# The stick-breaking mixer's logits from 64-row matmuls in pairs, copied from PSUM to SBUF before anything reads them

## The chip, the cores and the metric

The kernel runs on one NeuronCore of a Trainium2 chip. The metric is the device time of one launch in microseconds (us). The kernel before took 719.55 us (median of 3 runs, 719.12 to 720.17).

## The reference

One layer of a model on 512 tokens of width 1024, with 16 meta tokens ahead of them (528 keys). All numbers are float32. A projection by `w_in` feeds two mixers: a gated recurrence (`hgrn2`, 4 heads) and a stick-breaking attention (8 heads of width 64). Their outputs side by side go through `w_out`, then come a residual with layer norm, a mixture of 16 experts and a second layer norm. The part that is changed is this, for blocks of 128 queries:

```
z = einsum('bhqd,bhkd->bhqk', q[start:end] * 64**-0.5, k[:end])      # logits, 8 heads
log_keep = where(mask, log_sigmoid(-z), 0)
log_a = log_sigmoid(z) + cumsum(log_keep, reverse=True) - log_keep
a = where(mask, exp(log_a), 0)
o = einsum('bhqk,bhkd->bhqd', a, v[:end])
```

After it `h = layer_norm(ALPHA * h + mixed @ w_out)`.

## The kernel before

The work falls into stages: the projections and the recurrence (up to about 243 us), the stick-breaking mixer woven with the multiplication by `w_out` (to about 352 us), routing (to about 420 us), and the experts, whose weights stream in to the end.

**Large matmuls** are made as three: an operand is split into a high part (a copy on ACT, rounded) and a low part (the difference, on DVE or POOL), and `mm3` (L126 to L130) adds three products. For `w_out` the split is in `wo_half` (L711): a raw MB arrives by a DMA that SP issues (L716), ACT copies it (L725), and `lo_sub` (L124 on DVE, L122 on POOL) makes the low part. `out_proj` (L818) then makes 24 matmuls of 128x512 for each of four blocks of rows with the first half of `w_out`, and as many with the second half. They go to PSUM banks named `z`.

**The mixer** (`stick_breaking`, L568) takes its queries in three units: unit 0 is the block of the last 128 queries against 528 keys, unit 1 the block before it against 400 keys, unit 2 the first two blocks together (144 and 272 keys, 416 columns). Each unit goes through four pairs of heads. For each head `sb_weights` (L484) makes the logits in a PSUM bank `pj` (there are four of these), adds the mask by a small bf16 matmul, and then runs

```
ll = Abs(z)                    ACT  L504, reads PSUM
cc = max(z, 0)                 DVE  L508 (for 2 heads of 8 ACT, L506), reads PSUM
ll = Ln(1 + Exp(-ll))          ACT  L509, L510
cc = scan(cc + ll), reversed   DVE  L513
cc = z - cc                    DVE  L515, reads PSUM: the bank is held until here
cc = Exp(cc)                   ACT  L516
```

`sb_values` (L521) transposes the weights (L529), copies them out of PSUM on DVE (L531) and multiplies by the values (L536), one pair behind; `sb_finish` (L539) adds the meta tokens (L544, L548), normalizes, and transposes the result (L561). The queries lie in eight tiles `sqZ`, one for each head: 128 rows, of which 64 hold the head and 64 are zero, so that a matmul against the 128 rows of a pair of heads' keys takes the one head. `ev_sq` (L386) fills them: eight memsets on POOL (L393), four scaled copies on DVE (L397) and four on ACT (L395).

**What sets the order.** The program is written as generators that `weave` interleaves: 0.8 steps of `out_proj` to one step of `stick_breaking`. A scheduler then lays the instructions of each engine into a fixed order by when it believes each can run; on the chip each engine keeps that order. Large tiles (`big_tile`, 8 KB a partition) come from one pool of 14 buffers in the order of the program, and are reused in turn. The two tiles of `sqZ`, the tiles of `svt`, the gains `gb`, and the raw and split tiles of `w_out` all come from it. The first seven loads of expert weights (L879, from a pool of their own that becomes free when the recurrence is done) are issued by `pump` ahead of the weave; each load after the third waits until the load three before it has landed.

Of the kernel before, what the change touches and what calls it, by code (L numbers as in the profile page):

```python
# [13 lines left out]
AF = mybir.ActivationFunctionType  # L14
OP = mybir.AluOpType
# [3 lines left out]
P = 128  # L19
# [34 lines left out]
HG_LEAD = 2.0  # L54
WO_RATIO = 0.8
EARLY = 2
RELU_SHARE = 2
ZS_BUFS = 3
AT_BUFS = 2
T_BUFS = 2  # L60
# [21 lines left out]
def hymba_kernel(ctx: ExitStack, tc: tile.TileContext, x, meta, w_in, lbnd, hgg, sbg, w_out, ln1g, ln1b,  # L82
                 wrg, brg, wre, bre, wg, wu, wd, ln2g, ln2b, out):
    nc = tc.nc
    V = nc.vector
# [28 lines left out]
    def big_tile(k, dt=F32, pool=None):  # L114
        return (pool or big).tile([P, 2048], dt, tag="b", name="b").rearrange("p (k n) -> p k n", k=k)
# [46 lines left out]
    def tt(tag="t", bufs=T_BUFS, n=528, parts=P):  # L162
        return att.tile([P, 528], F32, tag=tag, bufs=bufs, name=tag)[0:parts, 0:n]
# [27 lines left out]
    for i2 in range(2):  # L191
        xr_ = xr[i2]
        for i1 in range(2):
            i = 2 * i2 + i1
# [25 lines left out]
    for m in (16, 8, 4, 2, 1):  # L220
        t = upool.tile([P, P], I32, tag=f"lm{m}", bufs=1, name=f"lm{m}")
# [9 lines left out]
    identb = att.tile([P, P], BF, name="identb")  # L231
    maskb = att.tile([P, P], BF, name="maskb")
# [136 lines left out]
            yield 1  # L369


    skT, sqZ, svt = [], [], []
    vbd = att.tile([P, 512], F32, name="vbd")

    def ev_sk(c, acc):
# [8 lines left out]
            V.tensor_copy(skT[c][:, 0:NM], p_[:, c, :])  # L384

    def ev_sq(c, acc):  # L386
        if c % 2 == 0:
            t = big_tile(4)
            sqZ.extend(t[:, j] for j in range(4))
        for s in range(2):  # L390
            q_ = sqZ[2 * c + s]
            r, o = slice(64 * s, 64 * s + 64), slice(64 * (1 - s), 64 * (1 - s) + 64)
            nc.gpsimd.memset(q_[o], 0.0)  # L393
            if s:
                nc.scalar.activation(q_[r], acc[r], AF.Copy, scale=0.125)  # L395
            else:
                V.tensor_scalar(q_[r], acc[r], 0.125, None, op0=OP.mult)  # L397

    def ev_sv(i, acc):
        if i == 0:  # L400
# [78 lines left out]
    UNITS = (((3,), ((0, 528),), 528, ((0, 1, 2, 3),)), ((2,), ((0, 400),), 400, ((0, 1, 2, 3),)),  # L479
             ((0, 1), ((0, 144), (144, 416)), 416, ((0, 1), (2,), (3,))))  # L480

    relu = [0]

    def sb_weights(pr, s, am, qts, spans, n):  # L484
        h = 2 * pr + s
        pieces = []
        if n == 528:
            for a in range(2):
                z = pj()
                nc.tensor.matmul(z[:, 0:264], sqZ[h][:, 384:512], skT[pr][:, 264 * a:264 * a + 264],  # L490
                                 start=True, stop=not a)
                pieces.append((z, 264 * a, 264))
            nc.tensor.matmul(z[:, 136:264], identb, maskb, start=False, stop=True)
        else:
            z = pj()
            for i, (a, b) in zip(qts, spans):
                nc.tensor.matmul(z[:, a:b], sqZ[h][:, i * P:(i + 1) * P], skT[pr][:, 0:b - a],
                                 start=True, stop=False)
                nc.tensor.matmul(z[:, b - P:b], identb, maskb, start=False, stop=True)
            pieces.append((z, 0, n))  # L500
        ll, cc = tt(), tt("zs", ZS_BUFS)
        relu[0] += RELU_SHARE
        for z, a, w in pieces:
            nc.scalar.activation(ll[:, a:a + w], z[:, 0:w], AF.Abs)  # L504
            if relu[0] // 8 != (relu[0] - RELU_SHARE) // 8:
                nc.scalar.activation(cc[:, a:a + w], z[:, 0:w], AF.Relu)  # L506
            else:
                V.tensor_scalar(cc[:, a:a + w], z[:, 0:w], 0.0, None, op0=OP.max)  # L508
        nc.scalar.activation(ll[:, 0:n], ll[:, 0:n], AF.Exp, scale=-1.0)  # L509
        nc.scalar.activation(ll[:, 0:n], ll[:, 0:n], AF.Ln, bias=1.0)  # L510
        for a, b in spans:
            rv = slice(b - 1, a - 1 if a else None, -1)
            V.tensor_tensor_scan(cc[:, rv], cc[:, rv], ll[:, rv], 0.0, op0=OP.add, op1=OP.add)  # L513
        for z, a, w in pieces:
            V.tensor_sub(cc[:, a:a + w], z[:, 0:w], cc[:, a:a + w])  # L515
        nc.scalar.activation(cc[:, 0:n], cc[:, 0:n], AF.Exp)  # L516
# [50 lines left out]

    def stick_breaking():  # L568
        todo = []
        st = {}  # L570

        def drain():
            pr, qts, spans, prs, am, bank_, zz = todo.pop(0)
            if pr == prs[0]:
                st["o"] = bank_()
            sb_values(prs.index(pr), pr, prs, st["o"], zz, qts, spans)
            if pr == prs[-1]:
                sb_finish(am, st["o"], prs, qts)

        for qts, spans, n, groups in UNITS:  # L580
            for g, prs in enumerate(groups):
                am = att.tile([P, 2, P], F32, tag="am", bufs=3, name="am")
                if len(prs) < 4:
                    nc.gpsimd.memset(am, 0.0)
                for m, pr in enumerate(prs):
                    zz = []
                    for s in range(2):
                        zz.append(sb_weights(pr, s, am, qts, spans, n))
# [670 lines left out]
    for e in range(NE):  # L1259
        acc = [pj(), pj()]  # L1260
# [53 lines left out]
    rows = rr + list(oth)  # L1314
# [103 lines left out]
```

## Time and profile before

| what | value |
|---|---|
| median of the runs | 719.55 us (719.12 to 720.17) |
| profiled execution, its own time | 718.7 us |
| span of its trace | 717.0 us |
| PE busy | 656.4 us, 92% |
| DVE busy | 540.7 us, 75% |
| ACT busy | 425.5 us, 59% |
| DMA, mean over the span | 200 GB/s |

The profiled execution lies 1.7 us over its span and 0.85 us under the median. Busy shares over the whole span mix stages with different limits, so the stage from 243 to 352 us is what has to be read, engine by engine. A timeline gives the start of each instruction, its duration (for a matmul with a modelled end, so that matmuls overlap on paper and the distance of two starts is the better measure), and in brackets how long the engine stood idle before it and what released it.

### The profile page before, as it was taken

What the parts mean: (1) busy time and instruction counts of PE and PEld (TensorE: products, weight loads), DVE (VectorE), ACT (ScalarE), POOL (GpSimd) and SP (SyncE); (2) the same over time, 40 slices, a digit from 0 to 9 for tenths busy, and PEclk for the clock granted to TensorE, in tenths of its full rate; (3) what the DMA queues carried; (4) which work ended last, traced back from release to release, by engine and by line L of the source; (5) the groups of instructions that cost most, each with busy time, mean ns of one, the idle gap of its engine ahead of it and who ended that gap; (6) DMA issues with size and microseconds to landing.
All of it is one profiled execution on the core that took longest, in us unless ns stands there. A gap on an engine that the chain in (4) does not pass through costs nothing. (4 is left out here: it accounts for less than half of the span.)

```text
span 717.0 us, 9402 instructions
## 1 busy us (share of the span) xinstructions
PE 656.4 (92%) x3366; PEld 530.0 (74%) x3366; DVE 540.7 (75%) x847; ACT 425.5 (59%) x640; POOL 164.4 (23%) x179
## 2 busy tenths in 40 slices
PE   6999999999999999989977799999999999999970
PEld 5878878777877777778766588888778788787750
DVE  5333063666465796999786899999999999998995
ACT  5353243525262683855323588778587786897782
POOL 5100143343334100100110011413204142112213
PEclk9999999999999999999988799999999999999995
DMA  9431111030003780203676599999999999998612
GB/s 349 137 111 59 59 59 29 31 118 1 1 1 118 291 353 1 82 37 120 208 279 229 180 321 346 353 328 368 329 341 361 337 353 334 350 351 313 200 59 116
DMA packets 62308, 143.67 MB, mean 200 GB/s; under 512 B 7371, under 2 KB 7403, under 8 KB 62257
## 3 DMA queue, kind: packets, MB, share of 16 engines
q1 hardware_dynamic: 53600, 128.98, 49.8%
q0 software_dynamic: 5904, 12.82, 6.1%
q10 hardware_dynamic: 2752, 1.22, 0.8%
q8 instruction: 28, 0.46, 0.3%
q14 instruction: 24, 0.19, 0.1%
HBM read 137.01 MB, written 14.68 MB: 212 GB/s over the span
## 5 line engine op out<-in xcount | busy, mean ns | idle before, releaser
L903 DVE TENSOR_TENSOR b<-b 128x1024 fp32r<-128x1024 f32 x192 | 225.0, 1218 | 6.1 <-ACT b L902 5.7
L902 ACT ACTIVATE b<-b 128x1024 fp32r<-128x1024 f32 x192 | 189.0, 1054 | 14.1 <-PE pj L130 9.6
L128 PE MATMUL pj<-b 128*128 128x512 f32 x264 | 107.5, 409 | 0.8 <-ACT b L200 0.4
L129 PE MATMUL pj<-b 128*128 128x512 f32 x264 | 105.3, 399 | 0.6 <-DVE b L124 0.6
L130 PE MATMUL pj<-b 128*128 128x512 f32 x264 | 105.2, 398 | 0.0
L128 PE MATMUL pj<-b,xh 128*128 128x512 f32 x224 | 90.5, 405 | 0.2 <-ACT b L902 0.2
L129 PE MATMUL pj<-b,xl 128*128 128x512 f32 x224 | 88.2, 395 | 0.0
L130 PE MATMUL pj<-b,xh 128*128 128x512 f32 x224 | 87.5, 407 | 0.5 <-DVE b L903 0.5
L969 POOL DMA_INDIRECT xg<-h1d,idx x15 | 21.2, 1412 | 182.2 <-DVE gate L966 82.7
L128 PEld LDWEIGHTS pj<-b 128*128 128x128 f32 x264 | 50.3, 191 | 11.7 <-DVE b L201 0.8
L124 DVE TENSOR_TENSOR b<-b 128x1024 fp32r<-128x1024 f32 x24 | 33.1, 1392 | 33.8 <-ACT b L329 30.2
L130 PEld LDWEIGHTS pj<-b 128*128 128x128 f32 x264 | 50.3, 191 | 11.0 <-issue 0.5
L129 PEld LDWEIGHTS pj<-b 128*128 128x128 f32 x264 | 50.3, 191 | 10.6 <-DVE b L124 0.9
L1016 POOL DMA_INDIRECT ad<-y,idx x14 | 42.5, 3037 | 39.1 <-ACT b L902 28.3
L130 PEld LDWEIGHTS pj<-b,xh 128*128 128x128 f32 x224 | 42.7, 191 | 11.4 <-DVE b L903 2.6
L128 PEld LDWEIGHTS pj<-b,xh 128*128 128x128 f32 x224 | 42.9, 192 | 9.0 <-ACT b L902 1.5
L329 ACT ACTIVATE b<-b 128x1024 fp32r<-128x1024 f32 x28 | 29.3, 1055 | 33.8 <-PE pj L130 15.2
L129 PEld LDWEIGHTS pj<-b,xl 128*128 128x128 f32 x224 | 42.7, 191 | 8.7
L626 ACT ACTIVATE zs<-zs 128x512 f32<-128x512 f32 x28 | 17.7, 631 | 48.1 <-POOL zs L625 48.0
L122 POOL TENSOR_TENSOR b<-b 128x1024 fp32r<-128x1024 f32 x8 | 19.6, 2448 | 91.1 <-ACT b L329 71.5
L624 POOL TENSOR_TENSOR zs<-u 128x256 f32<-128x256 f32 x28 | 22.2, 793 | 65.2 <-issue 27.4
L627 DVE TENSOR_TENSOR zs<-zs,u 128x256 f32<-128x256 f32 x28 | 13.3, 474 | 25.0 <-ACT zs L626 25.0
(337 smaller groups left out, 1310.1 us busy)
## 6 DMA issues: line engine op xcount, KB each, us to landing
b<-in_w_exp_gate_dram SPq DMA_DIRECT2D x32, 1024.0 KB, 8.3
b<-in_w_exp_up_dram SPq DMA_DIRECT2D x32, 1024.0 KB, 9.7
b<-in_w_exp_down_dram SPq DMA_DIRECT2D x32, 1024.0 KB, 10.2
b<-in_w_in_dram SPq DMA_DIRECT2D x12, 1024.0 KB, 5.3
b<-in_x_dram SPq DMA_DIRECT2D x8, 512.0 KB, 7.6
b<-in_w_out_dram SPq DMA_DIRECT2D x4, 1024.0 KB, 5.0
b<-in_w_in_dram SPq DMA_DIRECT2D x4, 512.0 KB
h1d<-b POOLq DMA_DIRECT2D x4, 512.0 KB, 3.0
```

What stands on the lines that cost most here:

```text
L122: nc.gpsimd.tensor_sub(dst, src, hi)
L124: V.tensor_sub(dst, src, hi)
L128: nc.tensor.matmul(acc, ah, bh, start=first, stop=False)
L129: nc.tensor.matmul(acc, al, bh, start=False, stop=False)
L130: nc.tensor.matmul(acc, ah, bl, start=False, stop=last)
L329: latest[0] = nc.scalar.activation(wt[:, 0], src, AF.Copy).ins
L624: nc.gpsimd.tensor_sub(xv[:, :, 0, :], ref, bv[:, :, 0, :])
L626: nc.scalar.activation(X, X, AF.Exp)
L902: nc.scalar.activation(t[:, 0], raw, AF.Copy)
L903: V.tensor_sub(t[:, 1], raw, f32(t[:, 0]))
L969: nc.gpsimd.indirect_dma_start(out=dst, out_offset=None, in_=h1d, in_offset=bass.IndirectOffsetOnAxis(ap=idx, axis=0), bounds_check=T - 1, ...
L1016: nc.gpsimd.indirect_dma_start(out=ad, out_offset=bass.IndirectOffsetOnAxis(ap=idx, axis=0), in_=y, in_offset=None, bounds_check=T - 1, oo ...
```

## The change

The zero-padded tiles go: `ev_sq` copies a pair's queries (128 rows, both heads) to one tile `sqT` with one ACT instruction, four in all. A new `sb_logits` makes the logits of both heads of a pair, each with a matmul over that head's 64 rows of the array, in turn (head A, head B, then the masks); ACT copies each PSUM piece to SBUF (`zcs`, one more large tile, cut into three buffers of 528 columns). `sb_weights` then reads this copy for Abs, for max with 0 (always on DVE now), and for the subtraction, each in one instruction over the whole width.

```
     def ev_sq(c, acc):
-        if c % 2 == 0:
+        if c == 0:
             t = big_tile(4)
-            sqZ.extend(t[:, j] for j in range(4))
-        for s in range(2):
-            ...
-            nc.gpsimd.memset(q_[o], 0.0)
-            if s:
-                nc.scalar.activation(q_[r], acc[r], AF.Copy, scale=0.125)
-            else:
-                V.tensor_scalar(q_[r], acc[r], 0.125, None, op0=OP.mult)
+            sqT.extend(t[:, j] for j in range(4))
+        nc.scalar.activation(sqT[c], acc, AF.Copy, scale=0.125)
...
+    def sb_logits(pr, qts, spans, n):
+        rows = [slice(64 * s, 64 * s + 64) for s in range(2)]
...
+            for a in range(2):
+                z = [pj(), pj()]
+                for s, r in enumerate(rows):
+                    nc.tensor.matmul(z[s][:, 0:264], sqT[pr][r, 384:512], skT[pr][r, 264 * a:264 * a + 264],
+                                     start=True, stop=not a)
...
+        for s in range(2):
+            for z_, a, w in pieces[s]:
+                nc.scalar.activation(zc[s][:, a:a + w], z_[:, 0:w], AF.Copy)
+        return zc
...
-        for z, a, w in pieces:
-            nc.scalar.activation(ll[:, a:a + w], z[:, 0:w], AF.Abs)
-            if relu[0] // 8 != (relu[0] - RELU_SHARE) // 8:
-                nc.scalar.activation(cc[:, a:a + w], z[:, 0:w], AF.Relu)
-            else:
-                V.tensor_scalar(cc[:, a:a + w], z[:, 0:w], 0.0, None, op0=OP.max)
+        nc.scalar.activation(ll, zc, AF.Abs)
+        V.tensor_scalar(cc, zc, 0.0, None, op0=OP.max)
...
-        for z, a, w in pieces:
-            V.tensor_sub(cc[:, a:a + w], z[:, 0:w], cc[:, a:a + w])
+        V.tensor_sub(cc, zc, cc)
...
     def stick_breaking():
         todo = []
-        st = {}
+        st["zcs"] = big_tile(1)[:, 0]
```

The change also moves instructions that it does not touch. On SP, the queue that issues the loads of weights, this stood at the end of the projections before (`b_1914` and `b_1922` are the two raw tiles of the first half of `w_out`):

```order
L716 DMA b_1914<-in_w_out_dram 128x2x1024
L716 DMA b_1922<-in_w_out_dram 128x2x1024
L879 DMA b_1860<-in_w_exp_gate_dram 128x4x512
L879 DMA b_1862<-in_w_exp_up_dram 128x4x512
L879 DMA b_1864<-in_w_exp_gate_dram 128x4x512
L879 DMA b_1866<-in_w_exp_up_dram 128x4x512
L879 DMA b_1868<-in_w_exp_gate_dram 128x4x512
L879 DMA b_1870<-in_w_exp_up_dram 128x4x512
L879 DMA b_1872<-in_w_exp_gate_dram 128x4x512
L827 DMA b_1948<-in_x_dram 128x1024 x2
```

and this stands there now (`b_1900` and `b_1908` are the same two tiles):

```order
L885 DMA b_1847<-in_w_exp_gate_dram 128x4x512
L885 DMA b_1849<-in_w_exp_up_dram 128x4x512
L885 DMA b_1851<-in_w_exp_gate_dram 128x4x512
L885 DMA b_1853<-in_w_exp_up_dram 128x4x512
L885 DMA b_1855<-in_w_exp_gate_dram 128x4x512
L885 DMA b_1857<-in_w_exp_up_dram 128x4x512
L885 DMA b_1859<-in_w_exp_gate_dram 128x4x512
L722 DMA b_1900<-in_w_out_dram 128x2x1024
L722 DMA b_1908<-in_w_out_dram 128x2x1024
L833 DMA b_1940<-in_x_dram 128x1024 x2
```

The two loads of `w_out` moved behind all seven loads of expert weights. On ACT the high parts of `w_out` (L725) were made among the last head of the recurrence (L469 to L473, L463), ahead of the queries' copies (L395) and of the first Abs (L504):

```order
L469 ACTIVATE t<-oT 128x512
L725 ACTIVATE b<-b 128x1024
L472 ACTIVATE t<-z,eps_rms 128x512
L725 ACTIVATE b<-b 128x1024
L473 ACTIVATE t<-t 128x512
L463 ACTIVATE b<-t 128x512
L725 ACTIVATE b<-b 128x1024 x2
L395 ACTIVATE b<-pj 64x512 x2
L504 ACTIVATE t<-pj 128x264
```

Now they (L731) stand near the end of unit 0, among the copies of the logits (L506) and the functions of its last pair (L513 Abs, L515 and L516 Exp and Ln, L521 the last Exp):

```order
L506 ACTIVATE b<-pj 128x264
L513 ACTIVATE t<-b 128x528
L731 ACTIVATE b<-b 128x1024 x2
L521 ACTIVATE zs<-zs 128x528 x2
L506 ACTIVATE b<-pj 128x264 x2
L515 ACTIVATE t<-t 128x528
L513 ACTIVATE t<-b 128x528
L516 ACTIVATE t<-t 128x528
L515 ACTIVATE t<-t 128x528
L506 ACTIVATE b<-pj 128x400
L731 ACTIVATE b<-b 128x1024 x2
```

Ahead of the first two L731 stand 14 copies L506 and 23 of the other functions of unit 0. On PE the matmuls of `out_proj` (`z<-b`) began between the last projection and the first logits (L490):

```order
L129 MATMUL pj<-b 128x512
L130 MATMUL pj<-b 128x512
L128 MATMUL z<-b 128x512
L129 MATMUL z<-b 128x512
L490 MATMUL pj<-skT,b 128x264
L130 MATMUL z<-b 128x512
L490 MATMUL pj<-skT,b 128x264
```

Now they begin behind the first two logits of unit 1 (L497):

```order
L497 MATMUL pj<-skT,b 128x400
L500 LDWEIGHTS identb
L500 MATMUL pj<-maskb,identb 128x128
L497 MATMUL pj<-skT,b 128x400
L500 LDWEIGHTS identb
L500 MATMUL pj<-maskb,identb 128x128
L127 MATMUL z<-b 128x512
L128 MATMUL z<-b 128x512
```

Counted along PE's order, 42 of these matmuls stood before the first L497 and now none; 64 stood before the first L544 of unit 0 and now 56 (L549 now); 75 before its L561 and now 70 (L566 now); and 120 before unit 1's L544 in both. Behind that the two orders agree but for the mixer's own instructions.

## Rows read from the trace of the kernel before

**Rows 1.** Windows by stage: us, busy PE, PEld, DVE, ACT, POOL, clock, DMA share, GB/s.

```profile
243.00:268.00 25.00, 23.25 (x132) 18.00 (x130) 22.02 (x40) 20.75 (x46) 2.25 (x7) 1.00 0.97 383
268.00:310.00 42.00, 40.97 (x223) 31.65 (x224) 33.64 (x53) 26.27 (x51) 4.82 (x12) 1.00 0.16 51
310.00:352.00 42.00, 38.10 (x249) 31.97 (x247) 39.64 (x101) 21.87 (x48) 2.72 (x5) 1.00 0.27 87
440.00:717.00 277.00, 250.16 (x1182) 198.73 (x1180) 254.65 (x323) 206.45 (x259) 68.78 (x31) 0.96 0.86 301
```

**Rows 2.** Timeline of SP: start, us, line, out from in; loads are issued here.

```profile
228.61 3.90 SPq L716 DMA_DIRECT2D b<-in_w_out_dram  x2
238.85 0.37 SPq L879 DMA_DIRECT2D b<-in_w_exp_gate_dram  x1
...
251.76 0.37 SPq L879 DMA_DIRECT2D b<-in_w_exp_gate_dram  x1
252.24 1.87 SPq L827 DMA_DIRECT2D b<-in_x_dram  x4
```

**Rows 3.** DMA issues from 225 to 275 us: KB each, median us to landing.

```profile
b<-in_x_dram SPq DMA_DIRECT2D x4, 512.0 KB, 10.5
```

**Rows 4.** Timeline of PE through unit 0: start, us, line, out from in.

```profile
262.00 1.16 PE L490 MATMUL pj<-skT,b 128*128 128x264 f32 x4 [0.27 <-DVE zs L515]
...
269.05 0.47 PE L128 MATMUL z<-b 128*128 128x512 f32 x1
...
273.26 0.83 PE L497 MATMUL pj<-skT,b 128*128 128x400 f32 x2
```

**Rows 5.** Timeline of ACT through unit 0.

```profile
239.29 1.99 ACT L725 ACTIVATE b<-b 128x1024 fp32r<-128x1024 f32 x2
...
252.89 0.63 ACT L510 ACTIVATE t<-t 128x528 f32<-128x528 f32 x1
253.42 0.37 ACT L504 ACTIVATE t<-pj 128x264 f32<-128x264 f32 x1
253.69 0.38 ACT L506 ACTIVATE zs<-pj 128x264 f32<-128x264 f32 x1
...
271.96 0.65 ACT L516 ACTIVATE zs<-zs 128x528 f32<-128x528 f32 x1 [1.32 <-DVE zs L515]
```

**Rows 6.** Timeline of DVE, two scans one head apart in unit 0.

```profile
263.14 1.25 DVE L513 TENSOR_TENSOR_SCAN zs<-zs,t 128x528 f32<-128x528 f32 x1
...
266.25 1.24 DVE L513 TENSOR_TENSOR_SCAN zs<-zs,t 128x528 f32<-128x528 f32 x1
```

**Rows 7.** Timeline of PE from unit 0's end to unit 1's end.

```profile
282.97 0.28 PE L544 MATMUL tr<-ident,am 128*128 128x128 f32 x1
...
287.77 0.60 PE L561 MATMUL pj<-ident,t 128*128 128x128 f32 x4
...
313.67 0.52 PE L529 MATMUL tr<-ident,zs 128*128 128x128 f32 x3 [2.15 <-DVE aT L531]
...
315.55 0.28 PE L544 MATMUL tr<-ident,am 128*128 128x128 f32 x1
```

**Rows 8.** Groups by line: busy us, mean ns of one, idle before.

```profile
L497 PE MATMUL pj<-skT,b 128*128 128x400 f32 (+2 forms) x48 | 14.5, 408 | 0.0
L508 DVE TENSOR_SCALAR zs<-pj 128x400 f32<-128x400 f32 x6 | 3.4, 568 | 3.8 <-ACT t L504 2.9 <-PE tr L529 0.8
L605 DVE TENSOR_SCALAR u<-u,lbw 128x528 f32<-128x528 f32 x4 | 1.8, 492 | 0.0
```

**Rows 9.** Timeline of PE after an idle stretch, before the experts.

```profile
405.55 0.38 PE L955 MATMUL z<-vals,sel 128*128 128x5 bf16 x8 [4.16 <-DVEq L1094]
...
406.36 0.63 PE L129 MATMUL pj<-b 128*128 128x512 f32 x1
406.79 0.63 PE L130 MATMUL pj<-b 128*128 128x512 f32 x1
...
408.77 0.39 PE L129 MATMUL pj<-b 128*128 128x512 f32 x1
```

More of the change, by code (lines that the diff above doesn't have):

```diff
@@ L56 @@
 EARLY = 2
-RELU_SHARE = 2
 ZS_BUFS = 3
@@ L369, in projections @@
             yield 1
-    skT, sqZ, svt = [], [], []
+    skT, sqT, svt = [], [], []
     vbd = att.tile([P, 512], F32, name="vbd")
@@ L386, in ev_sq @@
     def ev_sq(c, acc):
-        if c % 2 == 0:
+        if c == 0:
             t = big_tile(4)
-            sqZ.extend(t[:, j] for j in range(4))
-        for s in range(2):
-            q_ = sqZ[2 * c + s]
-            r, o = slice(64 * s, 64 * s + 64), slice(64 * (1 - s), 64 * (1 - s) + 64)
-            nc.gpsimd.memset(q_[o], 0.0)
-            if s:
-                nc.scalar.activation(q_[r], acc[r], AF.Copy, scale=0.125)
-            else:
-                V.tensor_scalar(q_[r], acc[r], 0.125, None, op0=OP.mult)
+            sqT.extend(t[:, j] for j in range(4))
+        nc.scalar.activation(sqT[c], acc, AF.Copy, scale=0.125)
     def ev_sv(i, acc):
@@ L480, in hymba_kernel @@
              ((0, 1), ((0, 144), (144, 416)), 416, ((0, 1), (2,), (3,))))
[L482 to L486, printed above, removed]
+    st = {"zc": 0}
+    def sb_logits(pr, qts, spans, n):
+        pieces = [], []
+        rows = [slice(64 * s, 64 * s + 64) for s in range(2)]
+        zc = []
+        for s in range(2):
+            st["zc"] = (st["zc"] + 1) % 3
+            zc.append(st["zcs"][:, 528 * st["zc"]:528 * st["zc"] + n])
         if n == 528:
@@ L488, in sb_weights @@
             for a in range(2):
[L489 to L493, printed above, removed]
+                z = [pj(), pj()]
+                for s, r in enumerate(rows):
+                    nc.tensor.matmul(z[s][:, 0:264], sqT[pr][r, 384:512], skT[pr][r, 264 * a:264 * a + 264],
+                                     start=True, stop=not a)
+                    pieces[s].append((z[s], 264 * a, 264))
@@ L494, in sb_weights @@
+            for s in range(2):
+                nc.tensor.matmul(z[s][:, 136:264], identb, maskb, start=False, stop=True)
         else:
-            z = pj()
+            z = [pj(), pj()]
             for i, (a, b) in zip(qts, spans):
[L497 to L500, printed above, removed]
@@ L501, in sb_weights @@
-        ll, cc = tt(), tt("zs", ZS_BUFS)
-        relu[0] += RELU_SHARE
-        for z, a, w in pieces:
-            nc.scalar.activation(ll[:, a:a + w], z[:, 0:w], AF.Abs)
-            if relu[0] // 8 != (relu[0] - RELU_SHARE) // 8:
-                nc.scalar.activation(cc[:, a:a + w], z[:, 0:w], AF.Relu)
-            else:
-                V.tensor_scalar(cc[:, a:a + w], z[:, 0:w], 0.0, None, op0=OP.max)
-        nc.scalar.activation(ll[:, 0:n], ll[:, 0:n], AF.Exp, scale=-1.0)
-        nc.scalar.activation(ll[:, 0:n], ll[:, 0:n], AF.Ln, bias=1.0)
+                for s, r in enumerate(rows):
+                    nc.tensor.matmul(z[s][:, a:b], sqT[pr][r, i * P:(i + 1) * P], skT[pr][r, 0:b - a],
+                                     start=True, stop=False)
@@ new lines, in sb_logits, with sb_weights @@
+                for s in range(2):
+                    nc.tensor.matmul(z[s][:, b - P:b], identb, maskb, start=False, stop=True)
+            for s in range(2):
+                pieces[s].append((z[s], 0, n))
+        for s in range(2):
+            for z_, a, w in pieces[s]:
+                nc.scalar.activation(zc[s][:, a:a + w], z_[:, 0:w], AF.Copy)
+        return zc
+    def sb_weights(pr, s, zc, am, qts, spans, n):
+        h = 2 * pr + s
+        ll, cc = tt(), tt("zs", ZS_BUFS)
+        ll, cc = ll[:, 0:n], cc[:, 0:n]
+        nc.scalar.activation(ll, zc, AF.Abs)
+        V.tensor_scalar(cc, zc, 0.0, None, op0=OP.max)
+        nc.scalar.activation(ll, ll, AF.Exp, scale=-1.0)
+        nc.scalar.activation(ll, ll, AF.Ln, bias=1.0)
@@ L513, in sb_weights @@
             V.tensor_tensor_scan(cc[:, rv], cc[:, rv], ll[:, rv], 0.0, op0=OP.add, op1=OP.add)
-        for z, a, w in pieces:
-            V.tensor_sub(cc[:, a:a + w], z[:, 0:w], cc[:, a:a + w])
-        nc.scalar.activation(cc[:, 0:n], cc[:, 0:n], AF.Exp)
+        V.tensor_sub(cc, zc, cc)
+        nc.scalar.activation(cc, cc, AF.Exp)
         for m, (a, b) in enumerate(spans):
@@ L586, in stick_breaking @@
                     zz = []
+                    pieces = sb_logits(pr, qts, spans, n)
                     for s in range(2):
-                        zz.append(sb_weights(pr, s, am, qts, spans, n))
+                        zz.append(sb_weights(pr, s, pieces[s], am, qts, spans, n))
                         yield 1
```

## The prediction

> **What bounds the kernel now.** I read the windows by stage first. In the mixer's stage no single engine is full all the way, but PE comes nearest: 23.25 of 25 us in unit 0, 40.97 of 42 after it, then 38.10 of 42 while DVE has 39.64 [rows 1]. PE is so full because `out_proj` fills it: the mixer alone would leave it waiting. The timelines of DVE and PE show that in unit 0. DVE's scans come 3.11 us apart, one head each [rows 6], with something else between them all the time, and PE's logits wait for the subtraction that frees their bank (0.27 us, L515) [rows 4]. So DVE paces unit 0, and PE spends what is left over on `out_proj`. From 269 us on PE is itself the bound: 18 matmuls of `out_proj` run from 269.05 to 273.26, 0.234 us each, without a gap [rows 4]. Up to unit 1's end the only long stop is 2.15 us for a copy by DVE [rows 7]. The reader is to see two things: whatever `out_proj` work PE doesn't do in unit 0 it has to do later, and later there is little room.
>
> **The parts that cost little.** POOL's eight memsets and DVE's four copies of queries go, and ACT's copies stay four: at nothing, since they lie around the last projection, before DVE's cycle. DVE's max for one head becomes one instruction from SBUF instead of one or two from PSUM. The nearest rows are 0.568 us for 400 columns from PSUM and 0.492 for 528 from SBUF, another line [rows 8]; for unit 0 that is some 0.2 us a head, and the subtraction in one instruction perhaps 0.1 more. So DVE's cycle of 3.11 becomes about 2.85, 2 us less over unit 0's eight heads. Against it DVE now makes the low parts of `w_out` inside unit 0, three of about 1.2 us. I take unit 0 to end where it did, ACT's last Exp at 272 us [rows 5], within 2 us either way. ACT gets a copy for each piece and one Abs a head. Its pitch is 0.27 us for 264 columns and 0.53 for 528 [rows 5]; 24 more instructions of 0.4 to 0.53 us are 10 to 13 us, against slack of 42 - 26.27 and 42 - 21.87 us in the two later windows [rows 1]: nothing there, though in unit 0 ACT has only 4 us spare (25 - 20.75) and becomes as full as DVE.
>
> **The part that costs.** The static order of SP shows the two loads of `w_out` behind all seven loads of expert weights. Before, they were issued at 228.61 us and the experts' from 238.85; the seventh of these went out at 251.76, since each waits for the one three before, and right behind it came the blocks of `x`, 2 MB, which took 10.5 us to land [rows 2, 3]. The `w_out` loads now take the place of those 2 MB: issued at about 252.2, landed at about 262.7, where they used to be split on ACT by 241.3 (239.29 + 1.99) [rows 5].
>
> But ACT comes to them later still. It keeps its order, and ahead of the first two splits stand 14 copies (0.27) and 23 functions (0.55 with the gaps): 16.4 us. ACT starts on them at about 244.7; in the first two pairs it must wait for DVE's scan and subtraction, some 5 us by the 1.3 us that a last Exp waits [rows 5]. That gives 266, and two splits of 1.0 us make 268. On PE the matmuls of `out_proj` stand behind the second logits of unit 1; the bank of these is freed by a copy that stands behind those two splits and two Exps. So PE begins `out_proj` at about 270.5, with none done. Before, it had 42 done when it reached the first logits of unit 1 at 273.26 [rows 4].
>
> From there I count to unit 0's finish. Before, PE went from 273.26 to 282.97 with 22 matmuls of `out_proj` (64 - 42), two logits, and the transposes and values of the last heads. Now 56 stand there: 34 more at 0.234 us are 8.0 us; the two logits (1.4 us) are already done. 270.5 + 9.7 + 8.0 - 1.4 is 286.8; with the values of one more head or two behind (up to 2.6 us) 286.8 to 289.4, say 288.1: 5.1 us late. To L561 stand 14 instead of 11 matmuls, +0.7; to unit 1's finish 50 instead of 45, +1.2. If PE had no gap before, unit 1's finish would be 7.0 us late. It had 1.03 us (42 - 40.97) and then the 2.15 us stop [rows 1, 7], and the extra work fills these: 7.0 - 3.2 = 3.8 us late against 315.55 [rows 7].
>
> **Logits from half the rows.** In units 1 and 2 the 24 logits' matmuls cost at most 14.5 us on PE as recorded (48 passes, two for each float32 matmul) [rows 8]. Bounds: if the two heads of a pair ran wholly beside each other, 7.2 us would go; if not at all, nothing; and a change of the rows in use may cost something each time, where the trace has no row for it. The order on PE is both passes of head A, then both of head B, so at most the end of one can lie beside the start of the other: a quarter of it, 3.6 us, is what I take as the likely upper end. For a cost, the nearest is a logit's pitch itself, so I bound it by 0.3 us at each of about eight such groups, 2.4 us. The value I take is nothing, with -3.6 to +2.4 kept. The Trainium skill speaks against this part in the page TensorEngine Tiling (Array Packing), section Key Properties: a change of the tiling mode drains the engine. It gives no figure, and no row here shows a change of mode.
>
> Behind unit 1, unit 2's logits come in pairs too, so a second head's logits must be free before either's chain begins; this costs 0 to 2 us, I take 1. The experts behind 352 us follow the stage: their loads start as split weights free the buffers, DMA is 0.86 busy and DVE 254.65 of 277 us [rows 1], so nothing there gives the time back.
>
> **The sum.** 3.8 + 0 + 1.0 = 4.8 us. The profiled execution is 718.7 us, so 723.5; it lies 0.85 us under the median of 719.55, which gives 724.4 for the runs. I predict 724.5.
>
> **The clock.** With no `out_proj` in unit 0, PE stands idle for about 40% of it in pieces of 1 to 3 us. After an idle stretch of 4.16 us the trace shows matmuls 0.43 us apart until about 408.5 us and 0.23 after: 1.2 GHz, then 2.4 GHz [rows 9]. At the half clock through unit 0, the logits, transposes and values would take twice as long, but DVE paces them; what costs is a start of `out_proj` at the lower clock, about 1.5 to 3 us. It is in the range and not in the sum.
>
> **The rivals.**
>
> *A faster kernel (717 us).* PE's bank is free after the copy, not after the subtraction, so pairs of heads run ahead, and DVE gets its chain 2 us earlier in unit 0. If unit 0 ends 3 us earlier and the last two units, in which DVE is the fuller engine towards the end (39.64 of 42 [rows 1]), gain the 0.1 to 0.2 us a head for 16 heads, 2.5 us, this would outweigh the late `out_proj`. For it: the 0.27 us waits for L515. Against it: PE has the same `out_proj` work and no place to put it. 720 - 2.5 = 717.
>
> *Tiles wholly beside each other (720.5 us).* If head A's and head B's matmuls overlap fully, 7.2 us of PE go from the PE-bound part; DVE then bounds it, so no more than about 4 of them count: 724.5 - 4 = 720.5. Against it: the order A, A, B, B. The same page of the Trainium skill, same section, says that different tiles load weights and multiply in parallel. The trace of before has no such pair.
>
> *Low clock through the start of `out_proj` (730 us), slower still.* Place: PE from 270 to 280 us. Price: the 56 matmuls at 0.43 instead of 0.234 us for the first ten to fifteen, 2 to 3 us, and ACT and DVE full in unit 0, with the splits of `w_out` and their low parts between its functions, so that `out_proj` starts 3 us later: 724.5 + 5.5 = 730. It decides if PE's granted clock is under 0.7 when the first `z` matmul runs.
>
> *The move is not one.* If the splits came early enough after all, the sum is 0 to +1 and the time 720. The order on SP and ACT is fixed, so I give this little and count it with the second rival.
>
> **How the numbers follow.** The forecast 0.58, with its own range 721.5 to 728; the faster kernel 0.13; overlap or no move 0.13; the low clock 0.16. Faster or slower by over 0.2%, 1.4 us, is what a measurement of this kernel can tell from no change: 718.1 to 721.0 counts as the same. The faster rival gives faster 0.13. The overlap gives the same 0.11 and slower 0.02; the forecast's low end adds 0.03 to the same. That makes 0.13, 0.14 and 0.73. A range of 718.5 to 730.5 leaves out most of the faster rival and half of the low clock's.
>
> **What would show it.** In the profile of the changed kernel: `w_out` issued on SP at about 252 us behind seven loads; the first split on ACT at 264 to 268; the first `z` matmul on PE at about 270 instead of 243.6; PE some 10 us less busy in 243 to 268 and without a stop of 2 us before unit 1's finish, which is at 318 to 321; the routing shifted by as much as that finish. If the two logits of a pair start together, the overlap is real. I am wrong if unit 0's finish on PE (282.97 before) is not at least 3 us later, or if it is and the end of the stage isn't.

## The result and the profile after

The changed kernel took 738.11 us (median of 4 runs, 735.45 to 738.79) against 719.6 us for the kernel before: a ratio of 1.0242, 95% interval 1.0216 to 1.0268. It is slower, as forecast, but by 18.5 us where the sum had 4.8, and it lies outside the range of 718.5 to 730.5. The span of the profiled execution grew from 717.0 to 737.0 us.

The windows by stage, of the same stretches as [rows 1] and in the same columns:

```profile
243.00:268.00 25.00, 19.56 (x79) 13.29 (x78) 11.68 (x18) 17.22 (x38) 0.78 (x4) 0.68 1.03 403
268.00:310.00 42.00, 39.59 (x192) 30.11 (x192) 28.86 (x42) 22.21 (x45) 5.68 (x9) 0.87 0.15 54
310.00:352.00 42.00, 39.91 (x238) 30.09 (x236) 39.01 (x84) 30.61 (x63) 4.50 (x9) 0.96 0.21 76
```

The column to look at is the clock, the third number from the end. It was 1.00 in all three stretches before; now it is 0.68 and 0.87 in the first two. DVE, which paced unit 0, fell from 22.02 to 11.68 us of 25. The windows of 253 to 275 and 275 to 280 us show what bounds that stretch instead:

```profile
253.00:275.00 22.00, 21.66 (x75) 14.66 (x75) 14.34 (x20) 16.37 (x35) 2.54 (x6) 0.50 0.83 333
275.00:280.00 5.00, 5.00 (x16) 3.96 (x16) 0.00 (x0) 3.67 (x6) 1.27 (x2) 0.58 0.00 0
```

PE is busy for 21.66 of 22 us at half its clock, with nothing but the mixer's own small matmuls. The timeline of SP, to be held against [rows 2]:

```profile
248.17 0.37 SPq L885 DMA_DIRECT2D b<-in_w_exp_up_dram  x1
253.06 0.37 SPq L885 DMA_DIRECT2D b<-in_w_exp_gate_dram  x1
253.48 1.49 SPq L722 DMA_DIRECT2D b<-in_w_out_dram  x2
```

and the timeline of PE, to be held against [rows 4, 7]:

```profile
253.34 1.12 PE L534 MATMUL tr<-ident,zs 128*128 128x128 f32 x4 [5.44 <-ACT zs L521]
...
264.57 1.12 PE L534 MATMUL tr<-ident,zs 128*128 128x128 f32 x4
...
269.55 1.91 PE L541 MATMUL oT<-b,aT 128*128 128x64 f32 x8
271.40 1.70 PE L497 MATMUL pj<-skT,b 64*128 64x400 f32 x2
...
273.24 1.70 PE L497 MATMUL pj<-skT,b 64*128 64x400 f32 x2
...
274.92 0.78 PE L127 MATMUL z<-b 128*128 128x512 f32 x1
...
278.48 0.63 PE L127 MATMUL z<-b 128*128 128x512 f32 x1
278.91 0.51 PE L128 MATMUL z<-b 128*128 128x512 f32 x1
...
279.72 0.60 PE L534 MATMUL tr<-ident,zs 128*128 128x128 f32 x4
282.15 0.63 PE L534 MATMUL tr<-ident,zs 128*128 128x128 f32 x4 [1.84 <-DVE aT L536]
...
298.13 0.28 PE L549 MATMUL tr<-ident,am 128*128 128x128 f32 x1
...
331.49 0.42 PE L549 MATMUL tr<-ident,am 128*128 128x128 f32 x1
```

PE stood idle for 5.44 us while the first pair went through ACT and DVE. From then until about 279 everything runs at half speed: 11.2 us from one pair's transposes to the next pair's (253.34, 264.57), with the values of two heads and the logits of a pair and a half between them. The first matmul of `out_proj` comes at 274.92, and its matmuls are 0.43 us apart until about 279. Four transposes take 1.12 us at 264.57 and 0.63 at 282.15. The timeline of ACT shows the splits of `w_out` and the end of unit 0, against [rows 5]:

```profile
270.66 1.99 ACT L731 ACTIVATE b<-b 128x1024 fp32r<-128x1024 f32 x2
...
276.68 2.00 ACT L731 ACTIVATE b<-b 128x1024 fp32r<-128x1024 f32 x2
284.46 0.64 ACT L521 ACTIVATE zs<-zs 128x528 f32<-128x528 f32 x1 [5.79 <-DVE zs L520]
...
287.92 0.63 ACT L521 ACTIVATE zs<-zs 128x528 f32<-128x528 f32 x1
```

The last Exp of unit 0 starts at 287.92 instead of 271.96. Unit 0's finish on PE is 15.2 us late (298.13, before 282.97), unit 1's 15.9 (331.49, before 315.55), and unit 2's last transposes 18.7 (375.02, before 356.32). So four fifths of the loss are there by the end of unit 0.

### The profile page after: what moved, and what is told of

The parts are those of the page before. It is cut to its first block, busy times and chain, and to the rows that moved or that the text cites. A ratio compares the mean times of both kernels' runs of the same rounds, so it can differ in the third digit from the quotient of the medians.

```text
span 737.0 us, 9395 instructions
## 1 busy us (share of the span) xinstructions
PE 670.1 (91%) x3366; PEld 535.9 (73%) x3366; DVE 535.9 (73%) x835; ACT 431.4 (59%) x656; POOL 161.6 (22%) x171
## 5 line engine op out<-in xcount | busy, mean ns | idle before, releaser
L127 PE MATMUL pj<-b,xh 128*128 128x512 f32 x224 | 89.2, 399 | 0.2 <-ACT b L908 0.2
L129 PE MATMUL pj<-b,xh 128*128 128x512 f32 x224 | 86.6, 402 | 0.6 <-DVE b L909 0.5
L127 PEld LDWEIGHTS pj<-b 128*128 128x128 f32 x264 | 50.8, 193 | 11.3 <-DVE b L200 0.8
L128 PEld LDWEIGHTS pj<-b 128*128 128x128 f32 x264 | 51.0, 193 | 10.8 <-DVE b L123 0.9
L129 PEld LDWEIGHTS pj<-b 128*128 128x128 f32 x264 | 50.7, 192 | 11.1 <-issue 0.5
L328 ACT ACTIVATE b<-b 128x1024 fp32r<-128x1024 f32 x28 | 29.1, 1052 | 33.8 <-PE pj L129 15.2
L633 DVE TENSOR_TENSOR zs<-zs,u 128x256 f32<-128x256 f32 x28 | 15.0, 537 | 24.4 <-ACT zs L632 24.4
```

The source lines that it names most:

```text
L127: nc.tensor.matmul(acc, ah, bh, start=first, stop=False)
L128: nc.tensor.matmul(acc, al, bh, start=False, stop=False)
L129: nc.tensor.matmul(acc, ah, bl, start=False, stop=last)
L328: latest[0] = nc.scalar.activation(wt[:, 0], src, AF.Copy).ins
```

## The experiments

Two things were in dispute: whether the lost place of `out_proj` or the copy and the pairs make the time, and by which mechanism. "Early" below means that `out_proj` has its place of before, "late" that it has lost it.

| kernel | logits | copy | `out_proj` | ratio (95% interval) | first `z` | unit 0 finish | unit 1 finish | unit 2 last L561 | clock 243 to 268 |
|---|---|---|---|---|---|---|---|---|---|
| before | heads, 128 rows | no | early | 1 | 243.59 | 282.97 | 315.55 | 356.32 | 1.00 |
| e3_rows | pairs | no | early | 0.9969 (0.9946 to 0.9992) | 246.37 | 282.15 | 314.83 | 358.11 | 1.00 |
| e12_rows_again | pairs | no | early | 1.0012 (0.9985 to 1.0039) | 245.43 | 281.20 | 313.85 | 357.08 | 1.00 |
| e1_touch | pairs | yes | early | 1.0155 (1.0120 to 1.0190) | 246.77 | 282.96 | 316.65 | 366.90 | 0.99 |
| e8_heads | heads, 64 rows | yes | early | 1.0128 (1.0066 to 1.0189) | 247.57 | 283.11 | 313.85 | 366.73 | 1.00 |
| e2_late | heads, 128 rows | no | late | 1.0063 (1.0043 to 1.0083) | 268.40 | 288.74 | 321.94 | 362.71 | 0.86 |
| e6_rows_late | pairs | no | late | 1.0171 (1.0117 to 1.0226) | 269.79 | 291.14 | 324.22 | 366.13 | 0.64 |
| changed kernel | pairs | yes | late | 1.0242 (1.0216 to 1.0268) | 274.92 | 298.13 | 331.49 | 375.02 | 0.68 |
| e11_heads_late | heads, 64 rows | yes | late | 1.0366 (1.0317 to 1.0415) | 278.51 | 299.29 | 333.72 | 379.20 | 0.64 |

The starts are from PE's timeline of each profiled execution, the clocks from the windows.

**e1_touch: the place given back.**

```
             sqT.extend(t[:, j] for j in range(4))
+            nc.gpsimd.memset(t, 0.0)
...
         st["zcs"] = big_tile(1)[:, 0]
+        nc.gpsimd.memset(st["zcs"], 0.0)
```

This was to show why the loads had moved at all. Large tiles get their buffers in turn, and the first thing written to the old `sqZ` tiles was a memset that waited for nothing else. The first writes to `sqT` and `zcs` are copies of a projection's result and of the first logits. With two memsets added, the loads of `w_out` stand ahead of the experts' again (issued at 228.55 us).

> The changed kernel with one thing added: two memsets on POOL that write the tiles sqT and zcs as soon as their buffers are free, so that the loads of w_out stand ahead of the experts' loads again. Theory (out_proj's lost place makes the time): out_proj is back between the first logits, PE stays at the full clock in unit 0, and the time comes back to 715 to 722 us. Rival (the pairs and the copy make the chain of unit 0 longer by themselves): 730 us or more, unit 0 on PE still ends 10 us late.

Neither came true as a whole. Unit 0 ended where it did before, so the pairs and the copy cost nothing there; yet the time was 731.78 us. The timeline of PE and the window of 315 to 335 us:

```profile
282.96 0.28 PE L550 MATMUL tr<-ident,am 128*128 128x128 f32 x1
...
315.32 1.54 PE L542 MATMUL oT<-b,aT 128*128 128x64 f32 x6 [1.82 <-DVE aT L537]
316.65 0.42 PE L550 MATMUL tr<-ident,am 128*128 128x128 f32 x1
...
334.17 0.63 PE L129 MATMUL z<-b 128*128 128x512 f32 x1
...
336.27 0.39 PE L129 MATMUL z<-b 128*128 128x512 f32 x1
```

```profile
315.00:335.00 20.00, 19.46 (x79) 14.78 (x80) 13.86 (x34) 8.41 (x20) 1.65 (x3) 0.51 0.13 53
```

Unit 1 ends 1.1 us late, unit 2 10.6: in between PE ran at half its clock for 20 us, and full.

**e2_late: the lost place alone.**

```
-            nc.gpsimd.memset(q_[o], 0.0)
             if s:
-                nc.scalar.activation(q_[r], acc[r], AF.Copy, scale=0.125)
+                i_ = nc.scalar.activation(q_[r], acc[r], AF.Copy, scale=0.125)
             ...
+            with tc.issue_after(i_.ins):
+                nc.gpsimd.memset(q_[o], 0.0)
```

> The kernel before with one thing moved: each memset of sqZ stands behind the copy that fills the other half, so the tiles are first written only when the last projection is done; the mixer itself is as before. Theory (out_proj's lost place): w_out is loaded behind the seven loads of expert weights and the time goes up by 10 to 20 us, to 730 to 740. Rival (pairs and copy): 720 to 724 us, since the mixer is unchanged.

Between the two: 724.61 us, 4.3 over the 720.28 of the kernel before, measured beside it. The loads moved exactly as in the changed kernel, unit 0 ended 5.8 us late, unit 1 6.4. The window shows that the clock fell less here, 0.86:

```profile
243.00:268.00 25.00, 18.25 (x93) 14.63 (x92) 19.74 (x37) 18.84 (x39) 1.20 (x5) 0.86 1.03 402
```

**e3_rows, e12_rows_again: pairs without the copy, early.** `sb_logits` returns the PSUM pieces; Abs, max and the subtraction read them as before, and the tiles are written early.

```
-        for s in range(2):
-            for z_, a, w in pieces[s]:
-                nc.scalar.activation(zc[s][:, a:a + w], z_[:, 0:w], AF.Copy)
-        return zc
+        return pieces
```

> Logits from 64 rows in pairs, without the copy to SBUF: Abs, max and the subtraction read PSUM as before; the tiles are written early, so out_proj keeps its place. If the 64-row matmuls of a pair overlap in part (4 pitches of 0.44 instead of 0.67 us seen in the changed kernel's unit 1), 716 to 721 us; if the pairing holds both heads' banks too long, 722 to 730.

> The kernel of e3_rows again (64-row pairs read from PSUM, tiles written early) with more rounds: 717 to 720 us, a ratio of 0.995 to 0.999 if its gain is real.

719.28 and 719.82 us. The first interval lies below 1, that of the repeat holds 1: no difference that lasts.

**e4_copy: the copy with 128 padded rows.** `sqZ` stays and each head's pieces are copied to `zcs`, which is written early.

> Logits from 128 padded rows for each head as before, but copied to SBUF at once, and everything after reads the copy; out_proj keeps its place. If the copy only adds ACT work that has room, 717 to 721 us; if ACT becomes the bound of unit 0 (2.75 us of functions a head against DVE's 2.9), 721 to 726.

729.22 us, ratio 1.0121 (1.0092 to 1.0149). It tells nothing of the copy alone: three large tiles now lie ahead of `w_out`'s where there were two, the second load of `w_out` waited on SP to 242 us, the last two splits came at 247 and 254.6, and unit 0 ended at 291.60. e8_heads was made in its place.

**e5_fill: more work for PE in unit 0, late.**

```
+            d = zb()
+            for j in range(6):
+                nc.tensor.matmul(d, sqT[pr][:, 384:512], skT[pr][:, 0:512], start=True, stop=True)
```

> The changed kernel with six extra float32 matmuls of 128x512 after each pair's logits in unit 0, into a PSUM bank that out_proj doesn't use yet (their result is never read). Theory (PE without work in unit 0 falls to 1.2 GHz, and the mixer's own matmuls at that clock stretch unit 0): PE's clock stays above 0.9 in 243 to 268, unit 0's finish on PE comes back from 298 to 289 to 292, the time to 728 to 733 us. Rival (the pair's chain through ACT and DVE is as long at any clock): the added work only delays, 738 to 744 us.

749.88 us, ratio 1.0432 (1.0376 to 1.0488). A float32 matmul of 128x512 is two passes of 0.43 us in the trace, so that the 24 extra ones put 20.6 us of work on PE. Those of the last two pairs ran at 284.5 and 296.4 us, behind `out_proj`, whose banks they share, and the clock was 0.52 at 260 to 270. Neither theory is tested by it.

**e6_rows_late: pairs without the copy, late** (e3_rows without the two memsets).

> The 64-row pairs without the copy, and without the early writes of the tiles, so w_out comes behind the experts' loads as in the changed kernel. Theory (displaced out_proj costs 5 to 6 us as in the kernel before, and the copy makes the rest): 723 to 727 us. Rival (pairs alone, once out_proj is displaced, leave PE idle and at the low clock): 732 to 738 us.

731.06 us, nearer the rival: with `out_proj` gone, the pairs too leave PE idle (3.06 us at 248), and the clock falls to 0.64. But unit 0's finish is only 8.2 us late, and the clock is back at 264 us (but for 3 us from 267), before the first `z` matmul.

**e7_ratio: e1_touch with `WO_RATIO = 0.75`.**

> The changed kernel with the early writes (as in e1_touch) and WO_RATIO 0.75 for 0.8: 11 matmuls of out_proj stand behind unit 1's finish instead of before it, where PE fell to 1.2 GHz for 20 us. Theory (that fall is the whole of e1_touch's loss): the clock holds at 315 to 335 us and the time is 717 to 723 us. Rival (the copy and the pairs make unit 2's chain longer): 728 to 733 us.

726.76 us, ratio 1.0098 (1.0070 to 1.0126): between the two. The clock held (1.00 from 310 to 340 us) and unit 2 ended at 358.95 instead of 366.90, as the theory has it; but the order behind changed: the first matmul of the ranking in routing (`tr<-Mb,tri`) came at 372.16 instead of e1_touch's 364.57.

**e8_heads: the copy, head by head, early.** `sb_logits` takes one head, and `sb_weights` of that head follows.

> The changed kernel with the early writes, but the logits head by head: 64 rows, copied to SBUF, each head's functions right behind its logits. If the copy by itself makes the loss of e1_touch: 728 to 733 us. If the pairing of the copied heads makes it: 717 to 723 us.

729.01 us: the pairing isn't the cause of e1_touch's loss. Unit 2 ends as late as there (366.73), though the clock was 0.83 in 315 to 335 us and not 0.51. So the low clock can't be the whole of that loss either.

**e9_fill3, e10_fill4: again more work for PE in unit 0,** with `d = trb()` for `zb()` and three matmuls a pair, or four, four, three and three.

> The changed kernel with three extra float32 matmuls of 128x512 after each pair's logits of unit 0, into the bank of the transposes, where e5's stood behind out_proj for two of the pairs; PE's order is otherwise as in the changed kernel up to the last pair. They are 1.3 us at the full clock, and PE's first idle stretch is 5.4 us. Theory (low clock makes most of unit 0's 15 us): if the clock holds longer, unit 0's finish on PE comes earlier than 298 by 3 to 8 us, the time is 730 to 736 us. Rival (chain, whatever the clock): finish at 298 or later, 738 to 743 us.

> The same with four, four, three and three extra matmuls; some of out_proj's matmuls also stand before the values of the third pair here. Theory (low clock): granted clock in 243 to 268 above 0.9 and unit 0's finish at 288 to 292, the time 728 to 733 us. Rival (chain): finish at 298 or later, 738 us or more.

In e9_fill3 the clock held to 268 us. The window of 253 to 265 us of the changed kernel:

```profile
253.00:265.00 12.00, 11.66 (x40) 8.16 (x41) 6.36 (x10) 7.55 (x18) 0.59 (x3) 0.50 1.03 407
```

and of e9_fill3:

```profile
253.00:265.00 12.00, 11.78 (x64) 7.28 (x62) 9.77 (x15) 10.67 (x23) 0.48 (x2) 1.00 1.04 411
```

With extra work on it, PE gets through 64 matmuls instead of 40, and DVE through 9.77 us of work instead of 6.36. The extra work is larger than the expectation says: 24 passes of 0.43 us, six to a pair, 10.3 us in all. Unit 1's first logits came at 264.19 instead of 271.40, the last Exp of unit 0 at 278.28 instead of 287.92; of both, 1.6 us are that unit 0's first logits came earlier (242.69, in the changed kernel 244.30). But the time is 742.58 us, ratio 1.0316 (1.0285 to 1.0348), since the finish of unit 0 came only 3.2 us earlier (294.96): `out_proj` was waiting for its weights by then. (The profiled execution took 738.18 us, 4.4 less than the median.) The timelines of PE, DVE and POOL in e9_fill3:

```profile
277.62 1.23 PE L130 MATMUL z<-b 128*128 128x512 f32 x2 [3.55 <-DVE b L124]
```

```profile
274.26 3.30 DVE L124 TENSOR_TENSOR b<-b 128x1024 fp32r<-128x1024 f32 x1
```

```profile
273.45 3.04 POOL L122 TENSOR_TENSOR b<-b 128x1024 fp32r<-128x1024 f32 x1 [4.20 <-ACT b L735]
```

In unit 2 its clock fell again (0.67 at 330 to 340, 0.73 at 340 to 350). e10_fill4 held the clock less well (0.68 in 260 to 270) and finished unit 0 at 297.31: 741.19 us, ratio 1.0301 (1.0267 to 1.0334). So the two traces differ by 6 to 8 us in the mixer where the clock differs, in spite of the extra passes; but it is not shown that removing the low clock would give the kernel that time.

**e11_heads_late: the copy, head by head, late** (e8_heads without the two memsets).

> The copy to SBUF and 64 rows, but head by head, and without the early writes, so out_proj has lost its place. If the displacement costs the same 5 to 6 us as in the kernel before, on top of e8_heads' 9: 733 to 737 us with unit 0's finish at 289. If the pairing is what made unit 0 of the changed kernel so much longer than that, unit 0's finish is below 292; if the copy is, it is at 295 to 298 as there.

746.31 us: worse than all of it. The pairing is not at fault here either; PE ran at 0.50 from 250 to 280 us, and the first `z` matmul came at 278.51.

After these twelve runs it was open whether the copy's latency or the clock makes what e2_late doesn't; three more were to tell that.

**e13_abs, e15_abs_late: Abs reads PSUM, ahead of the copy,** early and late.

```
+            for z_, a, w in pieces[s]:
+                nc.scalar.activation(ll[:, a:a + w], z_[:, 0:w], AF.Abs)
             for z_, a, w in pieces[s]:
                 nc.scalar.activation(zc[s][:, a:a + w], z_[:, 0:w], AF.Copy)
```

> The changed kernel with the early writes, and with Abs reading PSUM ahead of the copy, so that the copy is no longer in the way of Exp and Ln. If the copy's latency in each pair's chain makes e1_touch's 11 us: 719 to 724 us. If the low clock at 315 to 335 us makes it, whatever the chain: 728 to 733 us with the same fall of the clock.

> The changed kernel with Abs reading PSUM ahead of the copy, and nothing else: out_proj has lost its place. If the copy's latency before the first Exp is what lets PE idle for 5.4 us and makes unit 0 so much longer than in e2_late and e6_rows_late: unit 0's finish at 291 to 293 and 730 to 734 us. If the low clock comes whatever the latency: finish at 296 to 299, 736 to 740 us.

e15_abs_late took 744.23 us, ratio 1.0339 (1.0283 to 1.0395), unit 0's finish at 302.63: with the copy behind Abs, no gain. The first transposes came 8.5 us behind the first logits (242.71, 251.18) where the changed kernel has 9.0 (244.30, 253.34), so the copy's place makes about half a microsecond of the first pair's chain. e13_abs took 726.53 us, ratio 1.0078 (1.0054 to 1.0101), between its two cases; its profile still has the clock at 0.66 in 315 to 335 us, so that copy and clock are not told apart by it.

**e14_fillu2: useless work at one place.** e1_touch with six extra matmuls where PE waited for DVE in unit 1's last pair.

```
+        if qts == (2,) and pr == 3:
+            d = pj()
+            for j in range(6):
+                nc.tensor.matmul(d, sqT[pr][:, 384:512], skT[pr][:, 0:512], start=True, stop=True)
```

> The changed kernel with the early writes and six extra float32 matmuls (2.6 us) between the transposes and the values of unit 1's last pair, where PE stood idle before its clock fell at 315 us in e1_touch. Theory (that fall costs unit 2 most of its 10 us): the clock holds in 315 to 335, unit 2 ends on PE at 358 to 362 instead of 366.9, the time is 720 to 726 us. Rival (the copy makes unit 2's chain longer): 730 to 734 us.

723.97 us, ratio 1.0044 (1.0020 to 1.0069), where e1_touch had 1.0155: about 8 us less time by the medians. The window of 315 to 335 us and the timeline of PE, against those of e1_touch above:

```profile
315.00:335.00 20.00, 19.95 (x128) 15.63 (x127) 17.64 (x45) 12.52 (x29) 1.65 (x3) 1.00 0.02 7
```

```profile
309.57 1.88 PE L543 MATMUL pj<-skT,b 128*128 128x512 f32 x4
...
312.24 2.74 PE L543 MATMUL pj<-skT,b 128*128 128x512 f32 x6
...
315.14 1.02 PE L543 MATMUL pj<-skT,b 128*128 128x512 f32 x2
...
317.52 0.28 PE L555 MATMUL tr<-ident,am 128*128 128x128 f32 x1
```

128 matmuls in the 20 us instead of 79. Unit 2 ended at 363.16 instead of 366.90, not at 358 to 362; this execution took 727.83 us, the median of the kernel is 723.97.

Two things keep this from being a clean test. The extra work is 12 passes of 0.43 us, 5.2 us and not 2.6. And the order changed with it: 109 matmuls of `out_proj` stand before unit 1's finish here, 120 in e1_touch, and 35 of them run in 315 to 335 us instead of 4. e7_ratio moved as many (109) and held the clock without any useless work. So the two runs show that unit 2 is shorter where the clock holds, but not that the useless matmuls held it.

**e16_rows_fill: pairs without the copy, early, with four such matmuls at each of two places.**

> The 64-row pairs read from PSUM with the tiles written early (as e3_rows), and four extra float32 matmuls ahead of the values of unit 1's last pair and of unit 2's first group, where PE stood idle by 1 to 2 us and its clock fell to 0.83 at 330 to 340 us. If what is left of the pairs' gain is lost there: 716 to 718.5 us, faster than the kernel before by 0.3 to 0.5%. If the extra matmuls are in the way of the values: 720 to 722 us.

722.99 us, ratio 1.0036 (1.0020 to 1.0051): with 16 extra passes, 6.9 us, the clock was 1.00 through the stage, unit 2 ended at 356.91 (357.08 in e12_rows_again, without them), and the kernel was no faster. None of the versions beats the kernel before beyond doubt.

## Why the prediction was wrong

**Right: where the first loss is; its size in part by luck.** The loads of `w_out` were forecast on SP at 252.2 us and went out at 253.48. e2_late makes this one change and costs 4.3 us, where the sum had 3.8 for it. But in its trace, of an execution that took 726.92 us, unit 1's finish is 6.4 us late and not 3.8, and the clock fell to 0.86 in 243 to 268, which the sum left out.

**Wrong: "DVE paces them".** That is the step that failed: in the part on the clock I let PE fall to 1.2 GHz in unit 0, took DVE to be the slower engine even then, and kept 1.5 to 3 us for a slow start of `out_proj`, in the range alone. But at the half clock PE took 11.2 us from one pair to the next, without a stop, where DVE's work for two heads is about 6 us (3.11 a head, [rows 6]). PE was the bound of unit 0 from 253 to 279 us. So the splits on ACT came at 270.66 instead of 266, the first `z` matmul at 274.92 instead of 270.5. Before it stood two logits of unit 1 that took 3.5 us (271.40 to 274.92) for the 1.4 that I counted at the full clock. The first dozen `z` matmuls took 4.8 us (274.92 to 279.72) for the 2.8 at full clock, and the transposes queued behind them, for which DVE then waited, put unit 0's finish at 298.13 instead of 288.1. Of these ten microseconds 4.4 are the later start of `out_proj`, 2.0 the slow dozen, 1.8 the stop before 282.15; the rest is smaller stops and the values of more heads than I counted behind 270.5. The rival of the low clock named the place, and its sign came true (0.50 up to the first `z` matmul); it priced the start of `out_proj` and ACT's delay at 5.5 us, and not the ten of unit 0 itself.

**Wrong in place: the copy at nothing.** With `out_proj` early, unit 0 and unit 1 end with the copy where they end without it: within 2 us of the kernel before in all five early kernels of the table. There the price of nothing holds. In unit 2 it doesn't: 366.9 and 366.7 with the copy, 356 to 358 without. In e1_touch much of this is again the low clock, which fell at a gap of 1.82 us where the kernel before kept it over one of 2.15 [rows 7]: with the clock held, unit 2 ended at 358.95 (e7_ratio) and 363.16 (e14_fillu2), both with the copy. In e8_heads the clock was low for a third of that time and unit 2 ended as late. e13_abs got about half of e1_touch's loss back with Abs ahead of the copy and a clock of 0.66 for 0.51. How much is the copy's latency, how much the clock and how much the order is not separated.

**The logits from half the rows: the bound right, the reason wrong.** The later units' 48 passes (L497) went from 14.5 us [rows 8] to 12.1. Four of these ran at the half clock; in e3_rows they take 10.9:

```profile
L497 PE MATMUL pj<-skT,b 64*128 64x400 f32 (+2 forms) x48 | 12.1, 475 | 0.0
```

```profile
L495 PE MATMUL pj<-skT,b 64*128 64x400 f32 (+2 forms) x48 | 10.9, 441 | 0.0
```

The 3.6 us less are the likely upper end that I gave, but not for its reason. I had both passes of head A run ahead of those of head B, so that at most a quarter of them overlapped. The timeline of PE has a pair of heads at 303.25 and a head by itself at 313.71:

```profile
303.05 0.27 PE L566 MATMUL pj<-ident,t 128*128 128x128 f32 x1
303.25 0.61 PE L497 MATMUL pj<-skT,b 64*128 64x400 f32 x2
...
304.13 0.29 PE L500 MATMUL pj<-maskb,identb 128*128 128x128 bf16 x2
...
313.71 0.94 PE L497 MATMUL pj<-skT,b 64*128 64x400 f32 x2
314.58 0.88 PE L541 MATMUL oT<-b,aT 128*128 128x64 f32 x6
```

The same place in the kernel before, with a head of 128 rows:

```profile
288.10 0.27 PE L561 MATMUL pj<-ident,t 128*128 128x128 f32 x1
288.21 0.50 PE L497 MATMUL pj<-skT,b 128*128 128x400 f32 x1
...
288.88 0.22 PE L499 MATMUL pj<-maskb,identb 128*128 128x128 bf16 x1
```

The first passes of the two heads start together at 303.25, and the four passes of both take 0.88 us; the two of one head alone take 0.87. So two heads that start together lie wholly beside each other, as the second rival had it, and not by a quarter. The gain is less than half because one head over 64 rows takes 0.87 us where over 128 rows it took 0.67 (288.21 to 288.88). And e3_rows and e12_rows_again show that the time gains nothing from it, so the rival's 4 us didn't come. That the Trainium skill's page TensorEngine Tiling (Array Packing), section Key Properties, has tiles run in parallel agrees with the 0.88. The same section of the Trainium skill has a change of the tiling mode drain the engine. A cost of a change shows here: the first 64-row pass comes 0.20 us behind the last transpose, where it came 0.11 behind it before (288.10, 288.21). That is 0.09 us, of the 0.3 by which I bounded it; whether a drain makes it no row says.

**DVE's gain** came as forecast, 0.2 us: max over 400 columns takes 0.359 us where it took 0.568 [rows 8]:

```profile
L514 DVE TENSOR_SCALAR zs<-b 128x400 f32<-128x400 f32 x8 | 2.8, 359 | 1.1 <-ACT b L506 1.1
```

It bought nothing in unit 0, since DVE no longer was the bound there. Behind the stage 1.3 us more were lost (20.0 of span against 18.7 at unit 2's end), as the forecast had the experts follow.

**What stays open.** Why the late kernels with a copy finish unit 0 at 298 to 303 us and those without at 289 to 291. Between e6_rows_late and the changed kernel it can be placed with the timeline of PE in e6_rows_late:

```profile
243.02 1.16 PE L485 MATMUL pj<-skT,b 64*128 64x264 f32 x6
...
249.77 1.12 PE L535 MATMUL tr<-ident,zs 128*128 128x128 f32 x4
...
262.31 2.54 PE L542 MATMUL oT<-b,aT 128*128 128x64 f32 x16
```

Of 7.0 us, 1.3 are there at the first logits (243.02 here, 244.30 in the changed kernel), 2.3 more at the first transposes (249.77, 253.34), 3.0 more at the end of the fourth head's values (264.85, 271.46), and 0.4 behind that. The 2.3 are the longer chain of a copied pair, of which e15_abs_late gives only half a microsecond back. In the 3.0 PE runs at the half clock in both, to 264 here and past the end there. Why the clock comes back in e2_late and e6_rows_late with nothing but the mixer on PE, and in the late kernels with a copy only behind `out_proj`'s first matmuls, the runs don't say. A part is the order, too: in e6_rows_late `out_proj` begins ahead of unit 1's logits, in the changed kernel behind two of them. A kernel that has the late place, the copy and the full clock throughout was not reached.

## What to carry to other kernels

A matmul stream that only fills gaps may also be what holds TensorE's clock up, as here: when an edit moves it away, price the engine's own small work at 1.2 GHz, and ask whether it then becomes the bound, before writing that another engine paces the stretch. Look first at the order of the instructions that the diff doesn't touch: what writes a pooled tile first decides when the tiles behind it get their buffers, and a memset that waits for nothing may be what lets a load go early. Where the clock falls at one gap, moving wide matmuls to it (e7_ratio) or adding some (e14_fillu2) took the ratio from 1.0155 to 1.0098 and 1.0044 here; compare the engine's whole order before saying which matmul did it, since the added ones moved eleven others.

## What the runs showed of the hardware

- The clock stayed at its lower level for long stretches with PE full: 21.66 of 22 us busy at 0.50 with 64-row logits, transposes and 64-column values, and 19.46 of 20 at 0.51 in e1_touch. In both it rose while matmuls of 128x512 ran (begun at 274.92 and 333.17, 0.43 us apart until about 279 and 335.8). But it rose in e2_late at 261 us with the mixer's 128-row logits, transposes and values alone. The windows of e2_late:

```profile
254.00:261.00 7.00, 7.00 (x30) 6.40 (x31) 5.08 (x10) 3.74 (x9) 0.42 (x1) 0.51 1.05 412
261.00:268.00 7.00, 5.57 (x37) 4.50 (x37) 6.38 (x13) 6.38 (x13) 0.39 (x2) 1.00 1.03 418
```

- Gaps of much the same length went differently: PE lost its clock in e1_touch after 1.82 us, behind 1.6 us of transposes and values, and kept it in the kernel before over 2.15 us that followed straight on `out_proj`'s matmuls [rows 7].
- A low part on DVE took 3.30 us while POOL made another for 3.04 us beside it (e9_fill3), and 1.2 us alone; it ended 1.1 us behind POOL's.
